# Biasing three heads instead of two on TensorE in a streaming logsumexp, with one head summed by ScalarE and seven by VectorE

## The chip, the cores and the metric

One core of one Trainium2 chip. The metric is the device time of one execution in microseconds (us), lower is better; medians of several executions are quoted. Before the change: 328.25 us (328.14 to 328.33).

## The reference

```python
# x: 8 x 2048 x 2048 float32, bias: 8 x 256 float32
x_heads = x.reshape(8, 2048, 8, 256).transpose(0, 2, 1, 3) + bias[None, :, None, :]
x_tiled = np.repeat(x_heads, 2, axis=2)           # each row twice
lse = logsumexp(x_tiled, axis=-1)                 # over the 256 values of a head
# out: 8 x 8 x 4096 float32
```

The input is 134.2 MB, the output 1 MB. Every element is read once, biased, exponentiated and summed with 255 neighbours.

## The kernel before

The rows are cut into 64 tiles of 128 partitions x 2 rows x 2048 columns (2 MiB), which turn in nine buffers `xt`. One queue, SyncE's, issues all loads; a load into a buffer waits until the last users of the tile nine before are done. The first 50 tiles, which the change concerns, run in the mode BULK:

```python
BULK = dict(pe=2, g0=4, late=True, fold=0)      # tiles 0 to 49
MIXED = dict(pe=1, g0=4, late=False, fold=0)    # tiles 50 to 60
PROMPT = dict(pe=2, g0=8, late=False, fold=0)   # tiles 61 to 63, row by row
```

The eight heads of a tile are shared out as follows. Heads 0 and 1 get their bias on TensorE (a bf16 matmul of a row of ones with the bias cut into three parts, and a matmul with the identity that adds x in PSUM); ScalarE takes their exponential out of PSUM and sums at once, one instruction per row and head:

```python
def put_bias(m, k0, k1):                 # one bank of PSUM for each row, four rotate
    ...
        nc.tensor.matmul(p, lhsT=ones3, rhs=each_row(b3, 0, n, kb - ka),
                         start=True, stop=False)
def add_x(m, t, k0, got):
    ...
        mm = nc.tensor.matmul(p, lhsT=ident, rhs=xts[t % NBUF][:, ka:kb, 0:n],
                              start=False, stop=True)
def sum_biased(m, t, k, p, mm, sums):
    for h in range(m["pe"]):
        c = h * Dh
        act = nc.scalar.activation(out=xts[t % NBUF][:, k, c : c + Dh],
                                   in_=p[:, c : c + Dh], func=ACT.Exp,
                                   accum_out=sums[:, k, h : h + 1])
```

Heads 4 to 7 get their bias on GpSimd (`g_add`, in place). ScalarE takes the exponential of heads 2 to 7 in one instruction; VectorE multiplies heads 2 and 3 by exp(bias) and sums all six:

```python
def later(m, t, k0, k1, sums, add):
    h0 = m["pe"] if m["late"] else m["g0"]
    v = xts[t % NBUF][:, k0:k1, h0 * Dh : D]
    done = exp_inplace(t, v, add)                       # ScalarE
    if m["late"]:
        n = (m["g0"] - h0) * Dh
        f = v[:, :, 0:n]
        mul = nc.vector.tensor_tensor(out=f, in0=f,
            in1=each_row(w_ps, h0 * Dh - W0, n, k1 - k0), op=ALU.mult)
        ...
    red = nc.vector.tensor_reduce(out=sums[:, k0:k1, h0:H],
        in_=v.rearrange("p k (h j) -> p k h j", j=Dh), op=ALU.add, ...)
```

From tile 50 on VectorE sums single heads with a multiply-and-add (`weigh`), so that the tail after the last load is short. That code is the same in both kernels, except for where a weight lies.

The softmax here doesn't subtract the row's maximum and nothing guards it: scores larger than these inputs give would overflow.

## Time and profile before

| | before |
|---|---|
| time, median of 3 | 328.25 us |
| span of the profiled execution | 326.5 us |
| DMA engines busy, second to last-but-two slice of 40 | 90% or more each |
| busiest compute engines | GpSimd 288.4, VectorE 286.4, ScalarE 278.5 us |
| mean granted clock of TensorE | 0.746 |

The first line of the page gives each engine's busy time, its share of the span and its number of records; the row under it is the clock that TensorE was granted in 40 equal slices of the span, in tenths of full speed.

```profile
PE 230.7 (71%) x391; PEld 67.5 (21%) x391; DVE 286.4 (88%) x318; ACT 278.5 (85%) x574; POOL 288.4 (88%) x88
PEclk9999698588967985597658778968987655555576
```

Four engines are busy 70 to 90% of the time, and none of these shares says what bounds the kernel; the DMA row, shown in the prediction, does. The clock row matters because TensorE is the engine that gets more work.

### The profile page before, as it was taken

Reading aid. Unit: us, or ns where it says so; the run is one execution under the profiler, and the core shown is the slowest. Engines: PE = TensorE matmul, PEld = TensorE weight load, DVE = VectorE, ACT = ScalarE, POOL = GpSimd, SP = SyncE. Lnnn points to the kernel's source line nnn. Section 1 sums busy time; section 2 is a strip of 40 time slices with the busy share of each in tenths; the row PEclk is TensorE's granted clock in tenths of the full one; section 3 lists DMA queues with packets and bytes.
Section 4 is the critical chain, followed back from the end, with each engine's and each line's share of the span. In section 5 each row is a group of like instructions: output and inputs, shape, how many; then the busy total and the mean of one; then the engine's idle time right before and its main releaser. Section 6 shows DMA issues by size and latency. Waiting matters only on the chain.

```text
span 326.5 us, 1959 instructions
## 1 busy us (share of the span) xinstructions
PE 230.7 (71%) x391; PEld 67.5 (21%) x391; DVE 286.4 (88%) x318; ACT 278.5 (85%) x574; POOL 288.4 (88%) x88
## 2 busy tenths in 40 slices
PE   6798857777677668967798666686667355575791
PEld 2122211212122212312222212212112101222220
DVE  0029999999999999989998999989998999999994
ACT  3279999798889888799889889899888988799995
POOL 7999899979999999999998999999998999999713
PEclk9999698588967985597658778968987655555576
DMA  8999999999999999999999999999999999999993
GB/s 292 432 434 424 433 430 424 432 426 428 430 428 427 430 430 425 428 434 426 423 432 427 422 435 428 426 434 426 426 433 426 428 432 422 417 421 422 422 386 105
DMA packets 11807, 135.41 MB, mean 415 GB/s; under 512 B 1361, under 2 KB 1489, under 8 KB 2833
## 3 DMA queue, kind: packets, MB, share of 16 engines
q1 hardware_dynamic: 11696, 135.27, 98.5%
q8 instruction: 3, 0.05, 0.1%
q14 instruction: 10, 0.08, 0.1%
q0 software_dynamic: 96, 0.00, 0.0%
q10 hardware_dynamic: 2, 0.01, 0.0%
HBM read 134.23 MB, written 1.05 MB: 414 GB/s over the span
## 4 chain that ended last, share of the span: by engine, by line
DMA 69%; DVE 10%; POOL 7%; ACT 7%; PE 6%; issue 0%; SPq 0%
DMA xt<-in_x_dram 67%; DVE R L274 7%; POOL xt L251 6%; ACT xt L257 5%; PE ps L217 4%; DVE xt L267 2%; DMA b<-bparts 2%; ACT xt L232 2%; PE ps L202 1%; DMA brow<-in_bias_dram 0%; POOL brest L165 0%; POOL brest L167 0%; POOL b L170 0%; PE tpair L330 0%; POOL bparts L164 0%
## 5 line engine op out<-in xcount | busy, mean ns | idle before, releaser
L251 POOL TENSOR_TENSOR xt<-xt,b_rep 128x2048 f32<-128x2048 f32 (+1 forms) x66 | 277.5, 4209 | 22.1 <-DMA xt<-in_x_dram 21.9
L217 PE MATMUL ps<-xt,ident 128*128 128x512 f32 (+1 forms) x244 | 175.7, 852 | 78.8 <-DMA xt<-in_x_dram 78.5
L257 ACT ACTIVATE xt<-xt 128x3072 f32<-128x3072 f32 (+3 forms) x91 | 185.7, 2062 | 20.2 <-POOL xt L251 19.3
L274 DVE TENSOR_REDUCE R<-xt 128x12 f32<-128x3072 f32 (+1 forms) x56 | 181.4, 3240 | 2.3 <-ACT xt L257 0.6
L232 ACT ACTIVATE xt<-ps 128x256 f32<-128x256 f32 x234 | 86.8, 394 | 11.2 <-PE ps L217 11.1
L267 DVE TENSOR_TENSOR xt<-xt,w_ps 128x1024 f32<-128x1024 f32 x50 | 60.9, 1218 | 32.7 <-ACT xt L257 32.6
L217 PEld LDWEIGHTS ps<-xt,ident 128*128 128x128 f32 x244 | 55.3, 256 | 152.8 <-DMA xt<-in_x_dram 111.2
L232 ACT ACTIVATION_READ_ACCUMULATOR xt<-ps 128x1 f32 x234 | 51.0, 220 | 0.0
L202 PE MATMUL ps<-b,ones 3*128 3x512 bf16 (+1 forms) x122 | 47.5, 457 | 2.8 <-ACT xt L232 1.6
L285 DVE CUSTOM_DVE_ANT_0 xt<-xt,w_ps 128x256 f32<-128x256 f32 x95 | 34.0, 417 | 0.3 <-ACT xt L257 0.3
L202 PEld LDWEIGHTS <-ones 3*128 3x128 bf16 x122 | 8.0, 97 | 82.1 <-issue 82.1
L274 DVE TENSOR_REDUCE R_last<-xt 128x4 f32<-128x1024 f32 x10 | 12.2, 1218 | 0.0
L301 POOL TENSOR_TENSOR xt<-xt,w_sb 128x256 f32<-128x256 f32 (+1 forms) x2 | 2.1, 1032 | 8.7 <-ACT xt L257 8.5
L340 ACT ACTIVATE res<-tpair 64x512 f32<-64x512 f32 x7 | 4.1, 588 | 3.5 <-PE tpair L330 3.4
L174 PE MATMUL w_ps<-brow,ones 1*128 1x512 f32 x6 | 6.0, 1109 | 1.3 <-ACT w_ps L186 1.3
L330 PE MATMUL tpair<-ident,R 128*64 128x128 f32 x14 | 3.8, 364 | 3.7 <-DVE R L274 3.7
L186 ACT ACTIVATE w_ps<-w_ps 128x512 f32<-128x512 f32 x3 | 1.7, 582 | 5.4 <-PE w_ps L174 5.4
L174 PE MATMUL ps<-brow,ones 1*128 1x512 f32 x4 | 3.7, 1089 | 2.5 <-DMA brow<-in_bias_dram 2.5
L285 DVE DVE_READ_ACCUMULATOR2_ANT R_last<- 128x1 f32 x63 | 5.3, 84 | 0.0
L180 ACT ACTIVATE b_rep<-ps 128x512 f32<-128x512 f32 x2 | 1.2, 597 | 3.6 <-PE ps L174 3.6
L285 DVE DVE_READ_ACCUMULATOR2_ANT R<- 128x1 f32 x36 | 3.0, 85 | 0.0
L351 PE MATMUL tpair<-ident,R_last 128*128 128x128 f32 x1 | 0.5, 477 | 3.6 <-ACT xt L232 3.6
(24 smaller groups left out, 18.0 us busy)
## 6 DMA issues: line engine op xcount, KB each, us to landing
xt<-in_x_dram SPq DMA_DIRECT2D x56, 2048.0 KB, 31.9
xt<-in_x_dram SPq DMA_DIRECT2D x14, 1024.0 KB, 21.0
xt<-in_x_dram SPq DMA_DIRECT2D x5, 256.0 KB, 11.3
out_dram<-res SPq DMA_DIRECT2D x1, 896.0 KB, 8.0
xt<-in_x_dram SPq DMA_DIRECT2D x2, 384.0 KB, 16.5
out_dram<-res_last SPq DMA_DIRECT2D x1, 128.0 KB, 1.7
b<-bparts POOLq DMA_DIRECT2D x3, 1.0 KB, 6.0
brow<-in_bias_dram ACTq DMA_DIRECT2D x1, 8.0 KB
```

The lines of the kernel that those rows point to most:

```text
L174: nc.tensor.matmul(dst, lhsT=ones, rhs=brow[:, c0:c1], start=True, stop=True)
L202: nc.tensor.matmul(p, lhsT=ones3, rhs=each_row(b3, 0, n, kb - ka), start=True, stop=False,)
L217: mm = nc.tensor.matmul(p, lhsT=ident, rhs=xts[t % NBUF][:, ka:kb, 0:n], start=False, stop=True,)
L232: act = nc.scalar.activation(out=xts[t % NBUF][:, k, c : c + Dh], in_=p[:, c : c + Dh], func=ACT.Exp, accum_out=sums[:, k, h : h + 1],)
L251: add = nc.gpsimd.tensor_tensor(out=v, in0=v, in1=each_row(b_rep, c - G0, D - c, k1 - k0), op=ALU.add)
L257: return on_x(t, nc.scalar.activation(out=v, in_=v, func=ACT.Exp), [after])
L267: mul = nc.vector.tensor_tensor(out=f, in0=f, in1=each_row(w_ps, h0 * Dh - W0, n, k1 - k0), op=ALU.mult,)
L274: red = nc.vector.tensor_reduce(out=sums[:, k0:k1, h0:H], in_=v.rearrange("p k (h j) -> p k h j", j=Dh), op=ALU.add, axis=mybir.AxisListTy ...
L285: ttr = nc.vector.tensor_tensor_reduce(out=v, in0=v, in1=w, scale=1.0, scalar=0.0, op0=ALU.mult, op1=ALU.add, accum_out=dst,)
L301: done = nc.gpsimd.tensor_tensor(out=v, in0=v, in1=w_sb[:, h0 * Dh - W1 : h1 * Dh - W1], op=ALU.mult)
L330: nc.tensor.transpose(out=tp[0:nr, k], in_=R[b][:, k].rearrange("p h n -> p (h n)"), identity=ident,)
L340: nc.scalar.activation(out=res[:, b], in_=tv, func=ACT.Ln)
```

## The change

Its intent: take one multiply by exp(bias) from VectorE and give it to TensorE as a third biased head, and take the summing of a head from ScalarE, which needs an instruction for every row and head, and give it to VectorE, which sums many heads in one instruction. The changed lines, cut to the core:

```diff
-BULK = dict(pe=2, g0=4, late=True, fold=0)
+BULK = dict(pe=3, acc=1, g0=4, late=True, fold=0)
-    ps = [pp.tile([P, MM], F32, name=f"ps{i}") for i in range(4)]
+    one_ps = pp.tile([P, MM], F32, name="one_ps")
+    pairs = [pp.tile([P, 2 * MM], F32, name=f"pair{i}") for i in range(2)]
+    ps = [p[:, c : c + MM] for p in pairs for c in (0, MM)]
 ...   # start: b_rep copied by VectorE instead of ScalarE; one exp for w_ps, not three
+    def late_heads(m, t, got, sums):          # got: one_ps and the halves of a pair
+        for h, p in enumerate(got[:-1]):
+            mm = nc.tensor.matmul(p, lhsT=ident,
+                rhs=xts[t % NBUF][:, :, h * Dh : (h + 1) * Dh], start=False, stop=True)
+        def pe_part():
+            for k in range(K):                # head 0: two sums, as before
+                act = nc.scalar.activation(out=xts[t % NBUF][:, k, 0:Dh],
+                    in_=got[0][:, k * Dh : (k + 1) * Dh], func=ACT.Exp,
+                    accum_out=sums[:, k, 0:1])
+            act = nc.scalar.activation(       # heads 1 and 2, both rows, no sum
+                out=xts[t % NBUF][:, :, Dh : m["pe"] * Dh].rearrange(
+                    "p k (h j) -> p h k j", j=Dh),
+                in_=got[-1].rearrange("p (h k j) -> p h k j", k=K, j=Dh), func=ACT.Exp)
 ...   # later(): the multiply covers head 3 alone, the reduction heads 1 to 7
+            h0 = m["acc"]
+            v = xts[t % NBUF][:, k0:k1, h0 * Dh : D]
 ...   # tile 50: one_ps is refilled with exp(bias) of heads 1 and 2
+            if t == T_PROMPT and c0 == 0:
+                spread(one_ps, V0, W0)
+                nc.scalar.activation(out=one_ps, in_=one_ps, func=ACT.Exp)
```

Per tile ScalarE issues two sums, one exponential of 1024 and one of 2560 elements instead of four sums and one of 3072. The next tile's bias matmuls are issued after these, not before. The bank of the summed head, `one_ps`, has no second copy to rotate with.

More of the change, by code (lines that the diff above doesn't have):

```diff
@@ L17 @@
 NBUF = 9
-BULK = dict(pe=2, g0=4, late=True, fold=0)
-MIXED = dict(pe=1, g0=4, late=False, fold=0)
-PROMPT = dict(pe=2, g0=8, late=False, fold=0)
-PROMPT_F1 = dict(pe=2, g0=8, late=False, fold=1)
-PROMPT_F2 = dict(pe=2, g0=8, late=False, fold=2)
+BULK = dict(pe=3, acc=1, g0=4, late=True, fold=0)
+MIXED = dict(pe=1, acc=1, g0=4, late=False, fold=0)
+PROMPT = dict(pe=2, acc=2, g0=8, late=False, fold=0)
+PROMPT_F1 = dict(pe=2, acc=2, g0=8, late=False, fold=1)
+PROMPT_F2 = dict(pe=2, acc=2, g0=8, late=False, fold=2)
 FOLD = 32
@@ L60 @@
     T = B * NBLK
-    CPE = 2 * Dh
+    T_PROMPT = STAGES[1][0]
+    CPE = BULK["pe"] * Dh
     MM = 512
-    W0, G0, W1, W2 = Dh, 4 * Dh, 6 * Dh, 7 * Dh
+    V0, W0, G0, W1, W2 = Dh, 3 * Dh, 4 * Dh, 6 * Dh, 7 * Dh
     sb = ctx.enter_context(tc.tile_pool(name="sb", bufs=1))
@@ L179 @@
         spread(ps[i], c, c + MM)
-        nc.scalar.activation(
-            out=b_rep[:, c - G0 : c - G0 + MM], in_=ps[i], func=ACT.Copy
-        )
+        nc.vector.tensor_copy(b_rep[:, c - G0 : c - G0 + MM], ps[i])
     for c in range(W0, W2, MM):
-        w = w_ps[:, c - W0 : c - W0 + MM]
-        spread(w, c, c + MM)
-        nc.scalar.activation(out=w, in_=w, func=ACT.Exp)
+        spread(w_ps[:, c - W0 : c - W0 + MM], c, c + MM)
+    nc.scalar.activation(out=w_ps, in_=w_ps, func=ACT.Exp)
     nc.scalar.activation(out=w_sb, in_=b_rep[:, W1 - G0 :], func=ACT.Exp)
@@ L192, in put_bias @@
     def put_bias(m, k0, k1):
+        if m["late"]:
+            pair = pairs[n_ps[0] % 2]
+            n_ps[0] += 1
+            got = [one_ps, pair[:, 0:MM], pair[:, MM : 2 * MM]]
+            for h, p in enumerate(got):
+                nc.tensor.matmul(
+                    p,
+                    lhsT=ones3,
+                    rhs=each_row(b3, h * Dh, Dh, K),
+                    start=True,
+                    stop=False,
+                )
+            return got + [pair]
         n = m["pe"] * Dh
@@ L226, in add_x @@
         return rows
+    def late_heads(m, t, got, sums):
+        mms = []
+        for h, p in enumerate(got[:-1]):
+            mm = nc.tensor.matmul(
+                p,
+                lhsT=ident,
+                rhs=xts[t % NBUF][:, :, h * Dh : (h + 1) * Dh],
+                start=False,
+                stop=True,
+            )
+            mms.append(on_x(t, mm, [loads[t, 0, 0]]))
+        def pe_part():
+            for k in range(K):
+                act = nc.scalar.activation(
+                    out=xts[t % NBUF][:, k, 0:Dh],
+                    in_=got[0][:, k * Dh : (k + 1) * Dh],
+                    func=ACT.Exp,
+                    accum_out=sums[:, k, 0:1],
+                )
+                last_uses[t].append(on_x(t, act, [mms[0]]))
+            act = nc.scalar.activation(
+                out=xts[t % NBUF][:, :, Dh : m["pe"] * Dh].rearrange(
+                    "p k (h j) -> p h k j", j=Dh
+                ),
+                in_=got[-1].rearrange("p (h k j) -> p h k j", k=K, j=Dh),
+                func=ACT.Exp,
+            )
+            on_x(t, act, [mms[-1]])
+        return pe_part
     def sum_biased(m, t, k, p, mm, sums):
@@ L269, in later @@
                 in0=f,
-                in1=each_row(w_ps, h0 * Dh - W0, n, k1 - k0),
+                in1=each_row(w_ps, m["pe"] * Dh - W0, n, k1 - k0),
                 op=ALU.mult,
@@ L283, in weigh @@
         c = h * Dh
-        w = w_ps[:, c - W0 : c - W0 + Dh] if c < W2 else w_sb[:, c - W1 : c - W1 + Dh]
+        if c < W0:
+            w = one_ps[:, c - V0 : c - V0 + Dh]
+        elif c < W2:
+            w = w_ps[:, c - W0 : c - W0 + Dh]
+        else:
+            w = w_sb[:, c - W1 : c - W1 + Dh]
         ttr = nc.vector.tensor_tensor_reduce(
@@ L396 @@
             if c0 == 0:
-                got = add_x(m, t, k0, bias_there)
-                if next_units:
+                if m["late"]:
+                    pe_part = late_heads(m, t, bias_there, sums)
+                else:
+                    got = add_x(m, t, k0, bias_there)
+                if next_units and not m["late"]:
                     bias_there = put_bias(*next_units.pop(0))
@@ L430, in pool_part, with pe_part @@
                     load(t + NBUF)
-            def pe_part(t=t, m=m, got=got, k0=k0, k1=k1, sums=sums):
-                for k in range(k0, k1):
-                    sum_biased(m, t, k, *got[k - k0], sums)
+            if not m["late"]:
+                def pe_part(t=t, m=m, got=got, k0=k0, k1=k1, sums=sums):
+                    for k in range(k0, k1):
+                        sum_biased(m, t, k, *got[k - k0], sums)
             for_pool.append(pool_part)
@@ L439 @@
                     pe_part()
+                    if m["late"]:
+                        bias_there = put_bias(*next_units.pop(0))
                 else:
```

## The prediction

> **What bounds the kernel now.** I looked first at the activity of the DMA engines over the span and at the load queue's share, then at the chain of work that ended last.
>
> ```profile
> DMA  8999999999999999999999999999999999999993
> GB/s 292 432 434 424 433 430 424 432 426 428 430 428 427 430 430 425 428 434 426 423 432 427 422 435 428 426 434 426 426 433 426 428 432 422 417 421 422 422 386 105
> q1 hardware_dynamic: 11696, 135.27, 98.5%
> ```
>
> From the second slice to the last but two the sixteen DMA engines never rest, at 417 to 435 GB/s. The input is 8 x 2048 x 2048 x 4 bytes = 134.2 MB; at 428 GB/s that is 313.6 us of 326.5. A tile of 2 MiB passes in 2.097 / 0.428 = 4.90 us. So the question for every other engine is only whether it keeps below 4.90 us a tile, and what it does in the few us before the first byte and after the last.
>
> ```profile
> 290.06 19.82 DMA xt<-in_x_dram
> 309.90 10.19 DMA xt<-in_x_dram
> 320.12 0.63 ACT xt L257
> 320.76 0.63 ACT xt L257
> 321.38 1.47 ACT xt L232 x8
> 322.89 0.49 PE tpair L351
> 323.41 0.38 ACT res_last L357
> ```
>
> The end of the chain (start, duration, what): the last load lands at 320.1 us, and 6.4 us follow: two exponentials, four sums, a transpose, a logarithm, the store. All of it belongs to the last tile, whose code the change does not touch.
>
> ```profile
> xt<-in_x_dram SPq DMA_DIRECT2D x56, 2048.0 KB, 31.9
> SPq L135 <- DVE R L274: 230.1, 50, 18.1
> ```
>
> The first line (DMA issues) says that a load lands a median 31.9 us after its issue; the second (waits of the queue that issues loads) that an issue waits for VectorE's sum to free its buffer. Together: buffers come free late in order, but the queue still holds 31.9 / 4.90 = 6.5 tiles then. About five tiles, some 25 us, is how far the engines may fall behind before the DMA starves.
>
> ```profile
> L251 POOL TENSOR_TENSOR xt<-xt,b_rep 128x2048 f32<-128x2048 f32 x56 | 254.2, 4540 | 22.1 <-DMA xt<-in_x_dram 21.9 <-ACT w_ps L186 0.2
> L274 DVE TENSOR_REDUCE R<-xt 128x12 f32<-128x3072 f32 x50 | 167.7, 3354 | 1.7
> L257 ACT ACTIVATE xt<-xt 128x3072 f32<-128x3072 f32 x50 | 139.1, 2781 | 14.3 <-POOL xt L251 14.0
> L267 DVE TENSOR_TENSOR xt<-xt,w_ps 128x1024 f32<-128x1024 f32 x50 | 60.9, 1218 | 32.7 <-ACT xt L257 32.6
> ```
>
> Groups by form, of the first 50 tiles. GpSimd takes 4.54 us a tile and waits for loads; VectorE 1.22 + 3.35 = 4.57 us. ScalarE takes 2.78 us and, in the timeline, 1.55 us for its four sums: 4.33. All three are under 4.90.
>
> TensorE's cost per tile depends on its granted clock. Timeline of the first backlog (the same group of two input matmuls, four records):
>
> ```profile
> 15.32 3.78 PE L217 MATMUL ps<-xt,ident 128*128 128x512 f32 x4
> 20.00 3.78 PE L217 MATMUL ps<-xt,ident 128*128 128x512 f32 x4
> 24.44 1.98 PE L217 MATMUL ps<-xt,ident 128*128 128x512 f32 x4
> 26.89 1.98 PE L217 MATMUL ps<-xt,ident 128*128 128x512 f32 x4
> ```
>
> In this stretch PE is never idle, so starts give the full cost of two heads with their bias matmuls: 20.00 - 15.32 = 4.68 us slow, 26.89 - 24.44 = 2.45 us fast; that is 2.34 or 1.22 us a head.
>
> **What the Trainium skill says.** "DMA: Bandwidth & Descriptors", Measured, has 425 GB/s for 16 MB from HBM by one core alone, and the section on where 436 GB/s comes from derives a ceiling of 435.2. The slices agree (417 to 435): there is nothing left to win in the stream. "TensorE: Matmul & The Clock Gate", Part 1, says that the clock is half or full, that about 3.4 us of sustained work releases it and an idle window withdraws it. The trace agrees on the factor (3.78 against 1.98), less on the time: from 165 to 175 us PE was busy 9.71 of 10 us at a mean clock of 0.53. "ScalarE: Activation LUTs", What ACT_TABLE_LOAD costs, gives 186 ns plus 0.833 ns an element for an ACTIVATE with constant scale and bias. Here the rows for 3072 and 2048 elements (2781 and 1910 ns) give 0.851 ns an element and 168 ns fixed. "Perfetto Trace Analysis", Matmuls, advises rotating independent matmul groups through PSUM banks, so that evacuation overlaps the next group. Before, four banks rotate and PE waited for ScalarE to free one for 1.6 us in all; the change gives up part of this.
>
> **The change, part by part, for each of the 50 tiles.**
>
> *ScalarE.* Four sums of 256 (1.55 us) become two (0.78) and one exponential of 1024 from PSUM (168 + 1024 x 0.851 = 1.04). The large one shrinks from 3072 to 2560 elements: 2.78 - 512 x 0.00085 = 2.35. Sum 4.17 against 4.33: 0.16 us less, 8 us of busy time over 50 tiles. ScalarE is not the bound, so this is worth nothing directly.
>
> *VectorE.* The rows for 3072 and 2048 elements (3354 and 2286 ns) give 1.043 ns an element and 150 ns fixed. The product goes from 1024 to 512 elements: 684 ns. The reduction goes from six heads to seven, 3584 elements: 3888 ns. Sum 4.57 us, what it was: the work removed by the third biased head is put back by the two heads that ScalarE no longer sums.
>
> *TensorE.* Three heads: 3 x 1.22 = 3.66 us fast, 3 x 2.34 = 7.02 slow. This is the only engine that can pass 4.90. But a PE that is behind has no gaps, and in the trace it then became fast after some 9 us (15.3 to 24.4) and stayed so until it had caught up. A slow tile costs 2.1 us of lag, a fast one wins 1.2 back. An estimate: spells of up to 10 us, so 3 to 5 us of lag, against 25 us in the queue. PE busy rises from 230.7 to some 265 to 290 us.
>
> *The bank of the summed head* is single now: the order of instructions on PE is bias x3, input x3, and the next tile's first bias waits for ScalarE's two sums. Those start after the first input matmul, while PE does the other two. The shortest loop through it, fast, is two sums 0.75, three biases 0.8, one input matmul 1.0: 2.6 us, inside 4.90. It shows as a wait, not as time.
>
> *Start.* The bias is cut into three bf16 parts for 768 columns in place of 512 on GpSimd: casts 0.60 to 0.9, differences 1.14 to 1.7, together about 2 us later for the bias and GpSimd's first add. With three slow heads for the first tile (7.0 us in place of 4.7), VectorE begins about 4 us later than at 22.67. The first buffer came free at 27.3, when 9 - 27.3/4.9 = 3.4 loads (17 us) were still queued; now 13 us are. Not on the path. VectorE regains about 0.33 us a tile; it caught up near 97 us before and should near 150 us.
>
> *At tile 50* two weights are made by one matmul and one exponential more: 1 us of PE and 0.6 of ScalarE, once, within the queue's slack.
>
> Sum on the path: 0 us. Prediction 328.2 us.
>
> **The rivals.** (1) *TensorE becomes the bound.* For it: 7.02 us a tile at the slow clock, and stretches such as 165 to 175 that stay slow while PE is 97% busy. If half of the 50 tiles were slow in spite of full work, the mean were 5.34 us, 0.44 us over the DMA, 22 us of lag; the queue would swallow nearly all, and any rest would show in the time: up to 5 us, 333. If all were slow, 50 x 2.1 = 106 us less 25: 410. Against it: the backlog of the start was cleared at full speed, and idle gaps shrink, which should keep the clock up. (2) *VectorE's later start is carried to the end.* Its slack is small (4.57 of 4.90) and it is all but full from 260 to 318 us. If it were still several us behind in the last tiles, the tail would grow by what is left: 1 to 4 us, 329 to 332. Against it: from tile 50 on its work is 4.25 us a tile (starts at 271.14 and 275.38), so it gains 0.65 us a tile for eleven tiles more, and before it had caught up by 286 us. (3) *The lighter ScalarE shortens something.* If loads were held by buffers, 0.16 us a tile would give 8 us, 320. Against it: the queue is never empty, so an earlier release only makes a load wait longer in it. (4) *GpSimd slows down* because VectorE's product or reduction contends with it: it has 0.36 us a tile. The product, which reads two operands, gets shorter and has its weight in PSUM as before, so I see no cause.
>
> **Range and chances.** The stream and the tail are the same program, and the three runs before lie within 0.2 us. A small movement of the last stage in either direction is likelier than none, and rivals 1 and 2 only add: 327.5 to 329.3. Faster by 2% would need the stream to go beyond its ceiling: 0.01. Slower by 2% (334.8) needs rival 1 in earnest: 0.03. The rest, 0.96, is within 2%.
>
> **What would show it.** Right, if after the change the DMA row is 9 throughout at about 428 GB/s, the last load lands at 320 us within half a us, and the last 6.4 us hold the same instructions. ScalarE's busy time falls by about 8 us, VectorE's stays within 2, PE's rises by 35 or more; VectorE's first product starts near 26.5 us; the load's time from issue to landing falls a little below 31.9 us. It is wrong if slices with a DMA digit under 9 appear, with PE the releaser: then PE was the bound. If the stream is unchanged but the tail is longer with VectorE in it, rival 2 was right.

## The result

The changed kernel takes 327.59 us (median of 4, 327.31 to 327.81), against 328.25 (4 runs beside them, 328.14 to 328.33): a ratio of 0.998, interval 0.9962 to 0.9997. Ratios here are the mean time of one kernel's runs over the mean of the other's in the same rounds, so not quite the ratio of the medians quoted. Executions over 1.5% slower than the fastest of the same kernel are left out of the means. That is the same within 2%, and 0.66 us less. A later call, reported below, gave 327.55 for the changed kernel, 328.43 for a copy of the kernel before and 328.12 for that kernel's nine other runs beside them, so a gain of 0.57 or 0.88. The gain is small and two sets of runs of one kernel can lie 0.3 apart, but it repeats, and the prediction had 0.

The page of the changed kernel: its busy line, the clock row, the DMA rows and the issue row.

```profile
PE 250.0 (77%) x541; PEld 86.9 (27%) x541; DVE 285.9 (88%) x320; ACT 264.3 (81%) x421; POOL 289.9 (89%) x88
PEclk9999999899979979998997989797979855555558
DMA  8999999999999999999999999999999999999994
GB/s 293 427 431 429 431 429 424 431 427 429 429 429 429 427 426 429 429 423 430 432 425 429 431 422 427 431 427 429 429 431 425 429 432 424 413 422 421 422 400 143
xt<-in_x_dram SPq DMA_DIRECT2D x56, 2048.0 KB, 29.9
```

The stream is full in the same slices and at the same rate. TensorE was busy 19 us longer, at a clock that shows a 9 in 22 of the first 32 slices, before in 10. VectorE's busy time is unchanged, ScalarE's is 14 us less. A load lands 29.9 us after its issue, 2.0 earlier than before: the issues come later, because buffers come free later, and the queue is shorter for it.

Groups by form (count | busy, mean ns | idle time before, and what ended it):

```profile
L326 DVE TENSOR_REDUCE R<-xt 128x14 f32<-128x3584 f32 x50 | 194.4, 3888 | 1.7
L307 ACT ACTIVATE xt<-xt 128x2560 f32<-128x2560 f32 x50 | 117.7, 2354 | 9.5 <-POOL xt L301 9.3
L267 ACT ACTIVATE xt<-pair 128x1024 f32<-128x1024 f32 x50 | 52.3, 1045 | 17.2 <-PE pair L249 15.8
L319 DVE TENSOR_TENSOR xt<-xt,w_ps 128x512 f32<-128x512 f32 x50 | 34.0, 680 | 25.6 <-ACT xt L307 25.4
```

VectorE needs 680 + 3888 = 4568 ns a tile, before 1218 + 3354 = 4572. GpSimd's add, which nothing in the change touches, takes 4542 ns, before 4540. TensorE in the timeline, from one tile's first input matmul to the next one's:

```profile
32.36 1.12 PE L249 MATMUL one_ps<-xt,ident 128*128 128x512 f32 x2
33.33 1.88 PE L249 MATMUL pair<-xt,ident 128*128 128x512 f32 x4
35.50 0.37 PE L203 MATMUL one_ps<-b,ones 3*128 3x512 bf16 x1 [0.29 <-ACT xt L260]
35.71 0.59 PE L203 MATMUL pair<-b,ones 3*128 3x512 bf16 x2
36.23 1.12 PE L249 MATMUL one_ps<-xt,ident 128*128 128x512 f32 x2
```

A tile takes 36.23 - 32.36 = 3.87 us in the backlog of the start, under the 4.90 us of the DMA. The 0.29 in brackets is the wait for the single bank; in the view of waits it is 11.8 us in 27 waits, 1.0 at most:

```profile
PE one_ps L203 <- ACT xt L260: 11.8, 27, 1.0
```

And the end of the chain of work that ended last (start, duration, what), with VectorE's further steps of the same kind left out:

```profile
294.41 19.82 DMA xt<-in_x_dram
...
314.26 1.48 ACT xt L307
315.74 1.46 ACT xt L282 x8
317.20 1.47 ACT xt L307 x2
...
318.69 0.42 DVE xt L342
...
322.14 0.32 PE tpair L408
...
322.48 0.39 ACT res_last L414
```

The transpose starts at 322.14 instead of 322.89. It waits for the last sums of ScalarE and of VectorE. Before, ScalarE's ended last, 322.84 against VectorE's 322.62; now VectorE's, 322.00 against 321.67. Both branches moved earlier, by 1.2 and 0.6 us, because the loads they need landed earlier: the slowest of the sixteen landing signals of the last two pieces of x came at 318.81 and 319.45 us, before at 320.09 and 320.73. So the time was won in the stream, whose row looks the same. Why, the experiments had to say.

### The profile page after: what moved, and what is told of

Read it like the earlier page. It is cut to its first block, busy times and chain, and to the rows that moved or that the text cites. A ratio compares the mean times of both kernels' runs of the same rounds, so it can differ in the third digit from the quotient of the medians.

```text
span 325.5 us, 2113 instructions
## 1 busy us (share of the span) xinstructions
PE 250.0 (77%) x541; PEld 86.9 (27%) x541; DVE 285.9 (88%) x320; ACT 264.3 (81%) x421; POOL 289.9 (89%) x88
## 3 DMA queue, kind: packets, MB, share of 16 engines
HBM read 134.23 MB, written 1.05 MB: 416 GB/s over the span
## 4 chain that ended last, share of the span: by engine, by line
DMA 48%; DVE 33%; ACT 8%; POOL 6%; PE 3%; issue 1%; SPq 0%; DVEq 0%
DMA xt<-in_x_dram 45%; DVE R L326 27%; ACT xt L307 6%; DVE xt L319 4%; POOL xt L301 4%; DMA b<-bparts 2%; PE pair L249 1%; PE one_ps L249 1%; DVE xt L342 1%; ACT xt L282 1%; DMA brow<-in_bias_dram 1%; ACT xt L267 1%; POOL brest L173 1%; POOL brest L171 1%; PE pair L203 0%
## 5 line engine op out<-in xcount | busy, mean ns | idle before, releaser
L326 DVE TENSOR_REDUCE R<-xt 128x14 f32<-128x3584 f32 (+1 forms) x56 | 208.1, 3716 | 2.6 <-ACT xt L307 0.9
L307 ACT ACTIVATE xt<-xt 128x2560 f32<-128x2560 f32 (+3 forms) x91 | 164.2, 1828 | 14.8 <-POOL xt L301 14.3
L249 PE MATMUL pair<-xt,ident 128*128 128x512 f32 x200 | 105.5, 654 | 0.0
L249 PE MATMUL one_ps<-xt,ident 128*128 128x512 f32 x100 | 61.0, 695 | 19.9 <-DMA xt<-in_x_dram 19.8
L267 ACT ACTIVATE xt<-pair 128x1024 f32<-128x1024 f32 x50 | 52.3, 1045 | 17.2 <-PE pair L249 15.8
L249 PEld LDWEIGHTS pair<-xt,ident 128*128 128x128 f32 x200 | 42.4, 212 | 56.0 <-issue 56.0
L319 DVE TENSOR_TENSOR xt<-xt,w_ps 128x512 f32<-128x512 f32 x50 | 34.0, 680 | 25.6 <-ACT xt L307 25.4
L233 PE MATMUL pair<-xt,ident 128*128 128x512 f32 (+1 forms) x44 | 34.0, 872 | 21.2 <-DMA xt<-in_x_dram 18.2
L260 ACT ACTIVATE xt<-one_ps 128x256 f32<-128x256 f32 x100 | 37.7, 394 | 8.1 <-PE one_ps L249 8.1
L203 PE MATMUL one_ps<-b,ones 3*128 3x512 bf16 x50 | 19.0, 381 | 17.9 <-ACT xt L260 11.8
L203 PE MATMUL pair<-b,ones 3*128 3x512 bf16 x100 | 29.9, 378 | 0.0
L233 PEld LDWEIGHTS pair<-xt,ident 128*128 128x128 f32 x44 | 10.4, 294 | 29.6 <-DMA xt<-in_x_dram 19.7
## 6 DMA issues: line engine op xcount, KB each, us to landing
xt<-in_x_dram SPq DMA_DIRECT2D x56, 2048.0 KB, 29.9
```

Source lines behind the costliest of these rows:

```text
L203: nc.tensor.matmul(p, lhsT=ones3, rhs=each_row(b3, h * Dh, Dh, K), start=True, stop=False,)
L249: mm = nc.tensor.matmul(p, lhsT=ident, rhs=xts[t % NBUF][:, :, h * Dh : (h + 1) * Dh], start=False, stop=True,)
L260: act = nc.scalar.activation(out=xts[t % NBUF][:, k, 0:Dh], in_=got[0][:, k * Dh : (k + 1) * Dh], func=ACT.Exp, accum_out=sums[:, k, 0:1],)
L267: act = nc.scalar.activation(out=xts[t % NBUF][:, :, Dh : m["pe"] * Dh].rearrange("p k (h j) -> p h k j", j=Dh), in_=got[-1].rearrange("p ...
L307: return on_x(t, nc.scalar.activation(out=v, in_=v, func=ACT.Exp), [after])
L319: mul = nc.vector.tensor_tensor(out=f, in0=f, in1=each_row(w_ps, m["pe"] * Dh - W0, n, k1 - k0), op=ALU.mult,)
```

## The experiments

Twelve kernels ran, in three calls, each call on one chip with its own runs of the kernel before (medians 328.12, 328.28 and 328.12 us).

**Loads alone.** The program of the loads, with the compute taken out and constants stored (a wrong result).

```diff
-    (everything between the loads and the stores)
+    nc.vector.memset(res, 0.0)
+    nc.vector.memset(res_last, 0.0)
+    for t in range(T):
+        for k0, k1, c0, c1 in pieces(t):
+            nc.sync.dma_start(out=xts[t % NBUF][:, k0:k1, c0:c1], in_=rows_of(t)[:, k0:k1, c0:c1])
+    ...  # two stores, the last behind reads of the last tile
```

> A floor: the same loads in the same order and sizes, no arithmetic beyond clearing the result and copying a few elements of the last tile, so a wrong result on purpose. If the stream of loads sets the time, as predicted, this takes 322 to 325 us, at most 2% under the kernel before (the last load lands near 318 us). If the engines still cost several per cent of the time, it takes under 318. Second question, why the changed kernel is 0.66 us faster: in the trace of before the slowest of the 16 DMA engines finishes the last load 3.1 us after the middle one, in the changed kernel 1.4 us; I suppose that the fetches of instructions (packets of 8 and 16 KB, 0.3 and 1.1 us each, on one DMA engine at a time) make that distance. This kernel has next to no instructions: the supposition expects a distance under 1 us and the last load down by 2 us or more; if the distance is there without fetches, 2 to 3 us, the supposition falls.

Measured: 323.26 us, ratio 0.9848 (0.9834 to 0.9861). The end of its chain:

```profile
310.16 8.00 DMA xt<-in_x_dram
...
318.18 0.17 DVE res_last L165
```

And the row of its page with the instruction fetches of one of two such queues (packets, MB, share of the DMA engines), which will matter below:

```profile
q14 instruction: 1, 0.01, 0.0%
```

The stream sets the time: nothing in the kernel before can be worth more than 328.12 - 323.26 = 4.9 us. Of the spans' difference, 326.5 - 321.6 = 4.9, 2.6 lies before the last landing (320.73 against 318.16) and 2.3 in the tail after it. So some 2.6 us of a "full" stream are lost to something in the program. At this landing the slowest of the sixteen signals comes 0.77 us after the middle one, before 3.1, as the supposition about the fetches asked (under 1 us).

**More TensorE instructions.** The first guess: TensorE's 16 KB instruction fetches, visible as packets of a queue of their own, come at other moments in the changed kernel. Three one-column matmuls a tile, overwritten at once, give the kernel before the changed one's 541 records.

```diff
+            for i in range(TINY[ka] if m["late"] else 0):      # TINY = (2, 1)
+                nc.tensor.matmul(p[:, 0:1], lhsT=ones3, rhs=b3[:, 0:1], start=True, stop=True)
             nc.tensor.matmul(p, lhsT=ones3, rhs=each_row(b3, 0, n, kb - ka), ...)
```

> The kernel before with three matmuls of one column more per tile on TensorE, which bring its records per tile from 12 to 18, as in the changed kernel, and nothing else of the change. If the 0.66 us come from where the instruction fetches fall, TensorE's 16 KB fetches move from one in 99 us to one in 66 us as in the changed kernel, the distance of the slowest DMA engine changes, and the time moves by 0.3 us or more against before (to about 327.6 if TensorE's fetches alone decide it). If the gain comes from ScalarE's lighter work or from TensorE's clock, this stays within 0.15 us of 328.25 or rises.

Measured: 328.36 us, 1.0001 (0.9989 to 1.0014). The fetches moved from 99 to 116 us apart to 67 to 70, and the time did not change. The guess fell.

**VectorE over the limit.** The kernel before, with ScalarE summing one head of two and VectorE the other: VectorE then needs 1.21 + 3.89 = 5.1 us a tile, 0.2 over the DMA's 4.90. One theory was the prediction's: the queue of waiting loads absorbs some 25 us of lag. The other: lag at tile 50 has to be worked off afterwards, and only 0.65 us a tile can be.

```diff
             done = on_x(t, mul, [done])
+            h0 = 1
+            v = xts[t % NBUF][:, k0:k1, Dh:D]
         red = nc.vector.tensor_reduce(
 ...
+                if m["late"]:       # one head: two sums; the other: one exp of both rows
```

> One part of the change alone: two biased heads as before, but ScalarE sums one of them and VectorE the other. VectorE then takes 1.22 + 3.89 = 5.11 us a tile, over the 4.90 of the DMA, 0.54 us more than before: 50 x 0.54 = 27 us of work more before tile 50. If, as predicted, only a starved DMA queue costs time and some 25 us of lag are free, it takes 328 to 331 us. The rival: lag at tile 50 has to be won back by then by VectorE, which has only 0.65 us a tile to spare afterwards; VectorE would start at 23.5, end the 50th tile near 280 us instead of 262, and the kernel would take 338 to 343 us with DMA digits still 9 until late.

Measured: 340.5 us, 1.0367 (1.0351 to 1.0382). The DMA row of its page, and further down the shares of the chain by engine:

```profile
DMA  8999999999999999999999999999999999999800
...
DVE 91%; DMA 3%; PE 2%; POOL 1%; ACT 1%; issue 1%; DVEq 0%
```

The row is full to the 37th slice, so the DMA did not starve in the 50 tiles, as the prediction's theory has it; and yet 12 us were lost, at the end. VectorE waits once, for its first tile, and then works without rest. It leaves its 50th tile at 276.55 us, 13.9 later than in the kernel before (262.65). The prediction's theory falls: starving is not the only way to pay for lag. The other was right, though its 0.65 us a tile promised more: of the 13.9 us only some 1.5 were won back (12.4 lost). Why so little is said with the prediction below.

**TensorE over the limit, and just under it.** Two, then one, further identity matmuls a tile in the changed kernel, overwritten by the bias.

```diff
+            for i in range(2):                     # range(1) in the second kernel
+                nc.tensor.matmul(got[1 + i], lhsT=ident, rhs=b_rep[:, 0:MM], start=True, stop=True)
```

> The changed kernel with two more fp32 matmuls of 512 columns per tile in the first 50 tiles (results overwritten, so the output stays right): TensorE goes from 3.7 to 3.7 + 2 x 0.86 = 5.4 us a tile at full clock, over the 4.90 of the DMA. If 25 us of lag are free: 50 x 0.5 = 25 us are swallowed, 328 to 331 us. If lag has to be won back after tile 50 (9 us at most): TensorE ends its 50th tile near 18 + 50 x 5.4 = 288 us, and the kernel takes 342 to 352 us. TensorE being all but full, the granted clock should be over 0.9 in these tiles.

> One more fp32 matmul per tile for TensorE in the first 50 tiles of the changed kernel: 3.7 + 0.86 = 4.6 us at full clock, still under the 4.90 of the DMA, if the clock stays full; with slow spells the mean goes over it. Both readings of the slack expect nearly the same time here, 327.5 to 329.5 us; if the clock falls to half in a third of the tiles it is 335 or more.

With two: 355.81 us, 1.0837 (1.082 to 1.0853). With one: 327.38 us, 0.9971 (0.9957 to 0.9984). One tile of TensorE, two further matmuls first, then one:

```profile
206.11 1.13 PE L253 MATMUL one_ps<-xt,ident 128*128 128x512 f32 x2
...
211.35 1.12 PE L253 MATMUL one_ps<-xt,ident 128*128 128x512 f32 x2
```

```profile
33.57 1.12 PE L253 MATMUL one_ps<-xt,ident 128*128 128x512 f32 x2
...
37.95 1.12 PE L253 MATMUL one_ps<-xt,ident 128*128 128x512 f32 x2
```

5.24 us against 4.38, at nearly the same mean clock (0.906 and 0.908). The DMA's 4.90 lies between, and so does the step: above it 28 us are lost, below it nothing. With two, the loss is larger than either theory expected. The reason is the one just seen: VectorE leaves the 50th tile at 291.66 us, 29.9 later than in the changed kernel (261.75), and 28.3 of these (355.81 against 327.55) stay in the time. From there to the end of the span this kernel takes 62.8 us (354.5 - 291.66), the one with VectorE over the limit 62.7 (339.2 - 276.55), both with VectorE at the head of the chain; the kernels before and after, which wait for loads, take 63.9 and 63.8. So the slack at tile 50 is 1 to 1.6 us.

The prediction's 25 us did hold for what they were about. With two matmuls the loads first fall behind those of the changed kernel at 214 us, by 2.3 us, when VectorE is 24.2 us later than there (its 34th tile ends at 208.64, there at 184.44). Its last piece lands 6.1 us later (325.58 against 319.45), but the chain from tile 50 to the end is VectorE's.

**ScalarE's fetches.** ScalarE's instructions are fetched too, in 8 KB packets of 0.31 us. Of the packets in the trace I count as ScalarE's those that follow its record count; the others come at nearly the same times in all kernels. Before, they fall at its 46th, 183rd, 310th, 438th and 565th record: four by 241 us and a fifth at 318.5. After, at its 53rd, 177th and 320th: three. So the changed kernel has one fewer before the last large load, and a second one fewer before the last landing, because ScalarE has 421 records in place of 574. The fetch rows of the two pages, before and after, which count other engines' packets too:

```profile
q14 instruction: 10, 0.08, 0.1%
q14 instruction: 8, 0.07, 0.0%
```

That these packets are ScalarE's is an inference here; the last of the four kernels that tested it, in which ScalarE has nearly all the work, bears it out.

The kernel before with only the new start (four ScalarE instructions fewer), which should push the fifth fetch past the end:

```diff
-        nc.scalar.activation(out=b_rep[:, c - G0 : c - G0 + MM], in_=ps[i], func=ACT.Copy)
+        nc.vector.tensor_copy(b_rep[:, c - G0 : c - G0 + MM], ps[i])
 ...
+    nc.scalar.activation(out=w_ps, in_=w_ps, func=ACT.Exp)       # one, not three
```

> The kernel before with the changed kernel's start alone: VectorE copies the bias, ScalarE makes the weights in one exponential, so ScalarE has 4 instructions fewer and nothing else changes. Theory (instruction fetch): ScalarE fetches 8 KB of instructions every 127 to 128 of its instructions; in the kernel before the fifth fetch falls at 318.5 us, at its 565th of 581, beside the last two loads, and these two loads then land 1.33 us after the one before them in place of 0.66. Four instructions fewer move this fetch past 320.5 us, behind the last load; the time falls by 0.4 to 0.7 us, to some 327.6. Rival (the 50 tiles with three biased heads bring the gain, by less ScalarE work or a faster TensorE): no change, within 0.15 us of the kernel before.

Measured: 328.32 us, 0.9998 (0.9986 to 1.0011). The fetch did move, from 318.5 us to behind the last landing at 320.4 (two packets come then, at 321.9 and 327.2, and the trace doesn't say which of them is ScalarE's), and nothing was won. The fetch of the last few us alone doesn't make the 0.66 us.

The kernel before with 24 ScalarE records left out of tiles 20 to 22 (a wrong result):

```diff
+                if t in LEFT_OUT:                  # LEFT_OUT = (20, 21, 22)
+                    last_uses[t] += [mm for _, mm in got]
+                    return
```

> The kernel before with the sums of ScalarE left out in tiles 20 to 22 (24 of its instructions, counting the reads of the accumulator), a wrong result on purpose; near 100 to 115 us, where no engine is behind. Instruction fetch: the fetch at 318.5 us needs 24 instructions more than are left, so it does not come at all; 327.5 to 327.8 us. Rival: 12 us less ScalarE work in the middle of the kernel, off every path; within 0.15 us of the kernel before.

Measured: 327.99 us, 0.9989 (0.9977 to 1.0002). A miss: 0.29 us under the kernel before, between what the two theories expected, and no clear gain, with still four fetches before the last large load.

The changed kernel with 52 copies of one element on ScalarE before it starts, to make it four fetches again:

```diff
+    pad = sb.tile([1, PAD + 1], F32, name="pad")                 # PAD = 52
+    nc.vector.memset(pad, 0.0)
+    for i in range(PAD):
+        nc.scalar.activation(out=pad[:, i + 1 : i + 2], in_=pad[:, 0:1], func=ACT.Copy)
     for t in range(NBUF):
         load(t)
```

> The changed kernel with 52 copies of one element on ScalarE at the very start, where it waits for the bias. Instruction fetch: the fourth fetch of ScalarE, which would come at about its 453rd instruction and so never comes in the changed kernel, now falls near 313 us; the last loads land about 0.6 us later if it hits the slowest DMA engine, 328.0 to 328.3 us, and stay if it hits another (327.6). Rival: ScalarE's start is not on the path, 327.6. So a rise speaks for the fetch, no rise decides nothing.

Measured: 328.21 us, 0.9993 (0.998 to 1.0007), fetches at 8.6, 108.9, 211.1 and 304.0 us. On the same chip in the same rounds the changed kernel with one further matmul and three fetches took 327.38. The gain is gone, though TensorE, VectorE and the large ScalarE instructions work as in the changed kernel.

Last, the cost by itself: the loads alone, with 1280 copies of one element on ScalarE that nobody waits for.

```diff
+    for i in range(PAD):                                         # PAD = 1280
+        nc.scalar.activation(out=pad[:, i + 1 : i + 2], in_=pad[:, 0:1], func=ACT.Copy)
     for t in range(T):
         ...  # loads
```

> The loads alone (323.26 us, wrong result on purpose) with 1280 copies of one element on ScalarE, which nothing waits for: some ten more fetches of 8 KB of instructions. In the traces so far each such fetch put 0.4 to 0.7 us of delay on one of the 16 DMA engines, kept to the end. Instruction fetch: the slowest engine ends its loads 1 to 2.5 us behind the middle one in place of 0.8, and the time is 323.9 to 325.5. If a fetch costs a DMA engine only its own 0.3 us, or if fetches spread evenly, the distance stays near 1 us and the time under 323.7. If fetches are not the cause of the distance at all: 323.26 within 0.15.

Measured: 329.24 us against 323.26 of the loads alone (1.0032 and 0.9848 of the kernel before): 6.0 us, more than expected. Its fetch row, then the end of its chain:

```profile
q14 instruction: 12, 0.09, 0.1%
```

```profile
316.64 7.53 DMA xt<-in_x_dram
...
324.19 0.17 DVE res_last L172
```

0.09 MB among 135 go with 6 us. A load adds to its semaphore sixteen times, and the trace has the times. The Trainium skill ("DMA: Bandwidth & Descriptors", Why a DMA increments its semaphore by 16 and not by 1) says that each DMA engine that a load uses adds one; the sixteen times here agree with that. Sorted within each load, they show how far apart the engines are. How far the fastest, the second slowest and the slowest lag behind a steady beat of one load in 4.8945 us (my working from the trace, in us):

```
load ends   fetches so far   fastest   second slowest   slowest
  23.6            1            0.00         0.64          1.09
  29.1            2           -0.01         0.63          1.77
  39.6            3            0.02         0.64          2.47
  50.2            4           -0.02         0.63          3.30
  65.4            5           -0.02         0.63          3.83
  75.9            6           -0.01         0.62          4.53
  86.6            7           -0.02         0.61          5.37
```

It goes on to 5.90, 6.58 and 7.26 with the eighth to tenth, and stays there to the end: (7.26 - 1.09) / 9 = 0.69 us for each fetch, all on one of the sixteen, and never won back; the DMA row of this run is 9 from the second slice to the 38th, so the trace shows no pause in which it could be. Ten packets come in these loads, one for every 119 to 132 of ScalarE's records. The last large pieces ended at 319.6 on the second slowest and at 324.17 on this one. I had expected 323.9 to 325.5 for the time, because I took the fetches to be spread over the engines.

**Again, and the other way.** The changed kernel and the kernel before once more, and the changed kernel with ScalarE summing two of the three heads (so about five fetches):

```diff
-BULK = dict(pe=3, acc=1, g0=4, late=True, fold=0)
+BULK = dict(pe=3, acc=2, g0=4, late=True, fold=0)
 ...
+            for k in range(K):                     # a second summed head
+                act = nc.scalar.activation(..., in_=got[1][:, k * Dh : (k + 1) * Dh],
+                    func=ACT.Exp, accum_out=sums[:, k, 1:2])
```

> The changed kernel itself once more, beside a copy of the kernel before, for a second profile of both. If the order of fetches over the DMA engines is fixed by the program, the slowest DMA engine ends its last big loads again near 314.2 us (before: 314.9), 1.5 us behind the middle one (before: 2.5), and the time is 327.3 to 327.8. If the pattern is chance, the distances differ from the first profiles by a us and more.

> A copy of the kernel before, for its second profile: distance of the slowest DMA engine 2.3 to 2.7 us at the last big loads and a time within 0.15 us of the runs it is compared with, if the program fixes the pattern; a distance as in the changed kernel, 1.5 or less, if it is chance.

> The changed kernel with three heads biased by TensorE, but ScalarE summing two of them as before and taking the exponential of one: ScalarE 4.5 us a tile, VectorE 0.68 + 3.35 = 4.03 us. All under 4.90. The path theory of the prediction expects the time of the changed kernel, 327.4 to 328.3, though VectorE catches up by 60 us already. Instruction fetch: ScalarE has 200 records more than in the changed kernel, about two fetches more than before the change's three, so 327.9 to 328.5. If VectorE's lag of the start did cost something at the end: 327.0 or less.

Changed kernel: 327.55 us, 0.9982 (0.997 to 0.9995). Kernel before: 328.43 us, 1.001 (0.9997 to 1.0022), 0.31 over the nine other runs of the same kernel (328.12), where I had expected 0.15 at most. So 0.3 us between two sets of runs is nothing; the changed kernel is under both. The distances of the slowest from the middle signal came again, 2.5 and 1.4 us, so the program and not chance sets them. Two sums: its four fast runs 328.72 to 328.93, 1.0021 (1.0008 to 1.0035), 1.3 us over the changed kernel on the same chip, where two fetches more at 0.68 make 1.36; I had expected 327.9 to 328.5. Its VectorE work is smaller than the changed kernel's, so the loss is not VectorE's. The count of five comes from its 621 records and from two packets more in the fetch row (10, changed kernel 8), which is of a slow run.

That profiled run is a caution: 398.83 us, span 397.0. Busy line and clock row of its page:

```profile
PE 364.5 (92%) x541; PEld 104.7 (26%) x541; DVE 262.5 (66%) x320; ACT 287.6 (72%) x621; POOL 289.7 (73%) x88
...
PEclk9965555555555555555555555555555555555555
```

The clock stayed at half from the fourth slice on, although TensorE was busy 92% of the time and had 78% of the chain. That is the prediction's first rival, which I had priced at 410 us. It was one run of this kernel out of five and none of the changed kernel's (4 runs and 5).

## Why the prediction was right, and what it missed

*What bounds the kernel.* Right. Loads alone take 323.26 us, and the step at 4.90 us a tile was found between 4.38 (free) and 5.24 (28 us).

*VectorE, ScalarE by the instruction.* Right: 680 and 3888 ns measured, 684 and 3888 predicted; 1045 and 2354 measured, 1.04 and 2.35 us predicted. ScalarE's busy time fell by 14.2 us, not 8. By groups the sum was right: over the fifty tiles the large exponentials, the sums and the new exponential take 219.8 us before and 212.2 after, 7.6 less (a tile's four sums take 1.61 us on average and the two 0.85, predicted 1.55 and 0.78). The rest is what the sum left out. Records of successive instructions overlap, by 8.2 us in all before and 13.3 after, which takes 5.1 more off the busy time. Another 1.3 net is the start, whose copies moved to VectorE and whose exponentials merged, less the one at tile 50.

*TensorE.* The risk was judged rightly and the clock too low: 250.0 us busy, predicted 265 to 290. With fuller work the clock was higher (mean 0.859, before 0.746, with one more matmul 0.908), but full work doesn't ensure it: the slow run with two sums was busy throughout at 0.553. That none of the nine runs of the changed kernel fell into this may be luck in part. The single bank shows as a wait, as predicted.

*Start.* VectorE's first product came at 27.02 us (predicted near 26.5, before 22.67), and it first waits again at 153.9 (predicted near 150).

*How far engines may fall behind.* Wrong, without harm here. "About five tiles, some 25 us, is how far the engines may fall behind" is right for the starving of the DMA alone. What VectorE owes at tile 50 it must win back before the end, and the two kernels that owed 14 and 30 us won back 1.5 each. The gain of 0.65 us a tile that the second rival counts on for eleven tiles (7 us) comes in every kernel, but it is no reserve. The last fourteen tiles are 58.7 to 58.9 us of VectorE work in the kernels before and after and in the two that owed, 4.2 a tile against 4.90 of the stream. The kernel before already spends the difference: VectorE leaves tile 50 at 262.65, 7.1 us after that tile has landed, ends at 322.62, 1.9 us after the last landing, and waits only 1.0 us between the two. These waits are all that lag can use up. The changed kernel owed nothing, so the result stood. By the same measurement the first rival's "the queue would swallow nearly all" of 22 us was false comfort.

*The sum on the path.* Predicted 0, measured -0.66 us. The step that missed is "the last load lands at 320 us within half a us": it landed 1.3 us earlier, at 319.45. (The 320.1 us in the prediction is the last piece but one; the last landed at 320.73.) The missing term is ScalarE's instruction fetches, two fewer by then: the fourth, which comes before the last large load, and the fifth, at 318.5 us. The fourth first. The landing of the slowest and of a middle one of the sixteen signals for the same large load, the second row of tile 62, in nine kernels:

| kernel | ScalarE fetches by then | slowest, us | middle, us |
|---|---|---|---|
| before, first run and again | 4 | 314.86, 315.18 | 312.36, 312.70 |
| before with tiny matmuls, new start, fewer records | 4 | 314.81, 315.27, 314.79 | 312.58, 312.59, 312.68 |
| changed with 52 copies | 4 | 315.09 | 312.67 |
| changed, first run and again | 3 | 314.24, 314.17 | 312.78, 312.78 |
| changed with one further matmul | 3 | 314.14 | 313.10 |

With four fetches the slowest lands at 315.00 on average (314.79 to 315.27), with three at 314.18 (314.14 to 314.24), and the groups don't overlap. The middle engine isn't earlier in the changed kernel, so it isn't more bandwidth. A tenth kernel, VectorE over the limit, has ScalarE's instructions of the new kind with TensorE's old work, so 424 records and three fetches by then, and its loads were never held up: its slowest lands at 314.40, nearer to the three. From this landing to the end of the span all nine take 11.3 to 11.6 us. In the kernel before the slowest engine's lag can be followed fetch by fetch, 0.94, 1.62, 2.30, 3.00 us, and in the changed one 1.01, 1.69, 2.40. The engine that bore the fetches ends last, so the time goes with it.

The fifth fetch is worth less. With it the last piece but one lands 1.33 us after the piece before it, without it 0.65. But ScalarE's sums, which wait for these pieces, ended only 0.22 us after VectorE's, so no more than that can reach the end: 11.56 to 11.61 us in the three profiles of the nine that have it, 11.29 to 11.43 in the six that don't. This fits both misses: the kernel with the new start and the one with fewer records kept the four fetches and lost only the fifth, some 0.2 us, which is within the scatter.

The third rival, "the lighter ScalarE shortens something", I refused because it could only work through buffers. It came true by another way: not that ScalarE is done sooner, but that it has fewer instructions.

*What stays open.* Which of the sixteen engines it is, the trace doesn't say; in the two kernels it is inferred from sorted signals, and only the loads with copies show it beyond doubt. Why a packet of 0.31 us costs its engine 0.68 is not known. Before the first fetch the slowest engine is already 0.55 to 1.05 us behind the fastest, in two profiles of the same kernel 0.55 and 1.05, which may be why the times of one kernel scatter by 0.3. A program with still fewer ScalarE instructions was not run; I would expect the gain to end soon, since in the changed kernel another engine, hit by TensorE's 16 KB fetches, lags 1.96 us against 2.40. The changed kernel with one further, useless, matmul (327.38) isn't distinguishable from the changed kernel.

## What to carry to other kernels

When the DMA row is full, price every other engine by its time a tile against the DMA's, and check that what it owes at the end of the steady part can be won back before the end: a full DMA row doesn't show that debt. In this stream, which never rests, work moved between engines under the limit was worth nothing, but the number of ScalarE's instructions was worth something: their fetches rode on one of the sixteen DMA engines, 0.69 us each, which never made up for it and ended last. Count them before you call a change free. And an engine held just under the limit by a high clock is a risk that a median doesn't show.

## What the Trainium skill lacked or had wrong

- "Runtime: NRT & Kernel Launch", Instruction fetch mechanics, has instruction refills in 16 KiB blocks, "mostly hidden". TensorE's packets are 16 KB here, but ScalarE's are 8 KB, one for every 124 to 143 of its records. And hidden from the issuing engine is not free: beside a full stream each refill of ScalarE's cost one DMA engine 0.69 us that it never regained, 6.0 us for ten with the loads alone.
- No page says that all refills of one engine's instructions fall on the same DMA engine. The loads with copies show it: a lag of 7.26 us on one engine, of some 0.6 at most on the other fifteen while the fetches come.
- "TensorE: Matmul & The Clock Gate", Part 1, has some 3.4 us of sustained work as enough for the full clock; its nearest caveat is a clock seen stuck at a quarter for 50 us and more. One run here kept about half the clock for some 360 us at 92% busy (from 30 to 280 us busy without a break at a mean of 0.53), and took 398.83 us instead of 328.9.
- No page gives a way to tell how far an engine may fall behind a stream. 5.1 us a tile against 4.90 starved nothing and cost 12 us.
